# Full 128x128 stationaries for the small products of an RWKV-7 recurrence

## The chip, the cores and the metric

The kernel runs on one core of a Trainium2 chip. The metric is device microseconds of one execution, as the median of the runs. Matrix products run on TensorE (PE in the profile, its weight loads PEld), elementwise work on VectorE (DVE), ScalarE (ACT) and GpSimd (POOL); SyncE (SP) issues the DMAs.

## The reference

One hybrid decoder layer on 1024 tokens of width 1024, in float32: RMSNorm, one projection, a sliding-window attention branch and an RWKV-7 branch, both gated and merged, a hierarchical MoE and a last gated projection. The change touches the RWKV-7 branch, whose core is this scan over the tokens, for 8 heads of size 64:

```python
def step(state, inp):
    r_t, w_t, k_t, v_t, kk_t, a_t = inp
    sa = jnp.einsum('bhvk,bhk->bhv', state, -kk_t)
    state = (state * w_t[:, :, None, :]
             + sa[..., None] * (kk_t * a_t)[:, :, None, :]
             + v_t[..., None] * k_t[:, :, None, :])
    y_t = jnp.einsum('bhvk,bhk->bhv', state, r_t)
    return state, y_t
```

After it each head's output is normalised, scaled, gets a bonus term and is gated.

## The kernel before

The scan is done in chunks of 64 tokens, two chunks to a block of 128 tokens, 8 blocks. The 8 heads form 4 pairs `j`; in a pair, head `par` 0 lies on partitions 0 to 63 and head 1 on 64 to 127. `rwkv_block` (L654) writes for block `b`: the inputs of block b+1 (`rwkv_front`), chunk 0, the pairwise products of b+1 (`rwkv_pairs`, `rwkv_tokmajor`), chunk 1, the outputs (`rwkv_out`), and the inverse of b+1 (`rwkv_inverse`).

- `rwkv_pairs` (L469) multiplies `bk` with `stk`, masks the two PSUM banks into `ab` (two buffers) and `stk`, and sends the 16x16 diagonal blocks of `ab` (`xd`, `xc`) through DRAM to a forward substitution `T` (L503 to L507) and back as `dc`.
- `rwkv_inverse` (L538) makes the 64x64 inverse of each head and chunk in four rounds, (d,ab), (dt,e), (x,e), (x,e), each of 16 products with a 64x64 stationary, with an eviction by DVE between (L557, L566); the last gives `tt`.
- `rwkv_chunk` (L570) is the recurrence: z = stk.svu (8 products, stationary 128x64, L586), a copy `zs` by ACT, u = tt.zs (8, 64x64, L594), two copies of u into `svu`, the state pS = bkt.svu (8, 128x64, L602), `tmp` and the new `svu` by DVE, and the outputs: y1 = stk.svu (L589) and y2 = ab.svu (8, 64x64, L616), both into PSUM banks `py`, two for a block.
- `rwkv_out` (L618) reads `py` with DVE, normalises, transposes `yc` with 4 PE transposes and writes `yrT`.

A product in float32 shows as two MATMUL records, each with a weight load of its own. Between the small products `fill(n)` (L221) takes n steps of a generator of large products, three records each of 128x512 (`ps_mm<-h,wh` and `h,wl`, later `yah`, `yal`): the numbers of steps stand in `FN` (L30), 28 steps to a block. What is left of the generator runs after the last block (`branch_b`, L835). The Tile framework's scheduler makes a fixed order for each engine from priorities (program order, with the chunks pulled forward by `TN`) and the dependences; the engines then run in that order. PSUM tiles have tags with two buffers each: `mm`, `w`, `c`, `py`.

Of the kernel before, what the change touches and what calls it, by code (L numbers as in the profile page):

```python
# [37 lines left out]
_o = 0  # L38
# [8 lines left out]
for _n, _c in (("ident", 128), ("msk", 128), ("offm", 64), ("offt", 64), ("dm", 64), ("ind2", 2), ("i16", 256), ("tri", 128),  # L47
               ("bones", 128), ("band", 256), ("invf", 32)):
    CA[_n] = slice(_o, _o + _c)
    _o += _c  # L50
NCA = _o
CB = {}
# [19 lines left out]
class Kern:  # L72
# [157 lines left out]
    def rope_tables(self, pool):  # L230
        nc = self.nc
        MAGIC = 12582912.0
        n = 256
        pi = pool.tile([128, 8], I32, name="pos_i")
        nc.sync.dma_start(pi, self.a["positions"].rearrange("(t p) -> p t", p=128))
        pf = pool.tile([128, 8], F32, name="pos_f")
        nc.vector.tensor_copy(pf, pi)
        r = pool.tile([128, 8, 32], F32, name="rp_r")
        k = pool.tile([128, 8, 32], F32, name="rp_k")
        kh = pool.tile([128, 8, 32], F32, name="rp_kh")  # L240
        invf = self.ca[:, CA["invf"]]
# [12 lines left out]
        nc.vector.tensor_scalar(r, r, lim, -lim, op0=ALU.min, op1=ALU.max)  # L254
        sn = self.cos_sin[:, :, 1, :]
        nc.scalar.activation(self.cos_sin[:, :, 2, :], r, AF.Sin)
        nc.vector.tensor_scalar(self.cos_sin[:, :, 1, :], self.cos_sin[:, :, 2, :], -1.0, None, op0=ALU.mult)
        nc.vector.scalar_tensor_tensor(k, r, -1.0, r, op0=ALU.mult, op1=ALU.max)
        nc.vector.tensor_scalar(k, k, -1.0, math.pi / 2, op0=ALU.mult, op1=ALU.add)
        nc.scalar.activation(self.cos_sin[:, :, 0, :], k, AF.Sin)  # L260

    def att_block(self, n, ap):
# [50 lines left out]
        band = self.ca[:, CA["band"]][:, 256 - nk:]  # L313
# [53 lines left out]
    def rwkv_front(self, b, rp):  # L367
# [77 lines left out]
        for par in range(2):  # L445
            h = slice(par * 64, par * 64 + 64)
            nc.vector.tensor_tensor(bk[h, :, :, par, :], v4(na)[h], ei[h], op=ALU.mult)
            nc.vector.tensor_tensor(bk[h, :, :, 1 - par, :], v4(kp)[h], ei[h], op=ALU.mult)
            nc.vector.tensor_tensor(stk[h, :, :, par, 0:64], v4(kk)[h], ex[h, :, :, 0:64], op=ALU.mult)
            nc.vector.tensor_tensor(stk[h, :, :, par, 64:128], v4(r)[h], ex[h, :, :, 1:65], op=ALU.mult)  # L450
# [18 lines left out]
    def rwkv_pairs(self, b, st, rp):  # L469
# [3 lines left out]
        ab = rp.tile([128, 2, 4, 128], F32, name="ab", bufs=2)  # L473
        msk = self.ca[:, CA["msk"]]
        mb = lambda q: msk[q, None, :].to_broadcast([64, 4, 128])
        hs = [slice(0, 64), slice(64, 128)]
        for c in range(2):
# [11 lines left out]
        st["ab"] = ab  # L489
        dA, dT = self.dA[b % 2], self.dT[b % 2]  # L490
        x = rp.tile([128, 2, 4, 64], F32, name="xd", tag="f", bufs=5)
        nc.vector.tensor_tensor(x, ab[:, :, :, 0:64], self.ca[:, CA["dm"]][:, None, None, :].to_broadcast([128, 2, 4, 64]),
                                op=ALU.mult)
# [3 lines left out]
        sa = rp.tile([64, 16, 16], F32, name="sa", bufs=1)  # L497
# [13 lines left out]
        dc = rp.tile([128, 16, 16], F32, name="dc", bufs=1)  # L511
# [26 lines left out]
    def rwkv_inverse(self, b, st, rp):  # L538

        nc = self.nc  # L540
        ab, dc = st["ab"], st["dc"]
        shp = [128, 2, 4, 64]
        bc4 = lambda m: self.ca[:, CA[m]][:, None, None, :].to_broadcast(shp)
        f = lambda p: p.rearrange("p (c a t) -> p c a t", c=2, a=4)
        heads = [(c, j, slice(par * 64, par * 64 + 64)) for c in range(2) for j in range(4) for par in range(2)]
        n = lambda name: rp.tile(shp, F32, name=name, tag="td", bufs=4)
# [5 lines left out]
        e = n("e")  # L552
        p = self.ptile("c")
        for c, j, h in heads:
            self.mm(f(p)[h, c, j, :], ab[h, c, j, 0:64], d[h, c, j, :])
        self.fill(FN["in0"])
        nc.vector.tensor_tensor(e, f(p), bc4("offm"), op=ALU.mult)  # L557

        x = dt
        for i in range(3):  # L560
            p = self.ptile("c")
            for c, j, h in heads:
                self.mm(f(p)[h, c, j, :], e[h, c, j, :], x[h, c, j, :])
            self.fill(FN["in1"])
            x = n("x") if i < 2 else rp.tile(shp, F32, name="tt", bufs=2)
            nc.vector.tensor_tensor(x, f(p), dt, op=ALU.add)  # L566
        tt = x
        st["tt"] = tt

    def rwkv_chunk(self, b, c, st, nxt, rp):  # L570
        nc = self.nc
        stk, ab, bkt, tt = st["stk"], st["ab"], st["bkt"], st["tt"]
        if c == 0:
            st["py"] = [self.ptile("py") for _ in range(2)]
        fy = [p[:, :256].rearrange("p (a v) -> p a v", a=4) for p in st["py"]]
        f = lambda p: p[:, :256].rearrange("p (a v) -> p a v", a=4)
        svu = st["svu"][c]
# [21 lines left out]
        if not last:  # L599
            pS = self.ptile("c")  # L600
            for j, par, h in heads:
                self.mm(f(pS)[h, j, :], bkt[c][:, j, par * 64:par * 64 + 64], svu[:, j, par, :])  # L602
# [6 lines left out]
            nc.vector.tensor_tensor(tmp, self.sm, f(pS), op=ALU.add)  # L609
            ns = st["svu"][1] if c == 0 else nxt["svu"][0]  # L610
            for par in range(2):
                h = slice(par * 64, par * 64 + 64)
                nc.vector.tensor_tensor(ns[h, :, par, :], tmp[h], fc[h].to_broadcast([64, 4, 64]), op=ALU.mult)
            nc.gpsimd.tensor_tensor(self.sm, tmp, fc.to_broadcast([128, 4, 64]), op=ALU.mult)
        for j, par, h in heads:
            self.mm(fy[par][out, j, :], ab[h, c, j, 64:128], svu[h, j, par, :], start=False, stop=j == 3, skip=True)  # L616

    def rwkv_out(self, b, st, rp):  # L618

        nc = self.nc  # L620
        fy = [p[:, :256].rearrange("p (a v) -> p a v", a=4) for p in st["py"]]
        g = lambda n: rp.tile([128, 4, 128], F32, name=n, tag="g", bufs=2)
        st8 = rp.tile([128, 8], F32, name="st8", bufs=2)
        yc = g("yc").rearrange("p a (q v) -> p a q v", q=2)
        s2 = st8.rearrange("p (a q) -> p a q", q=2)
        for par in range(2):
            nc.vector.tensor_reduce(s2[:, :, par], fy[par], op=ALU.add, axis=AX.X)
# [12 lines left out]
        for j in range(4):  # L640
            self.tr(p[:, j * 128:(j + 1) * 128], yc[:, j].rearrange("p q v -> p (q v)"))
# [102 lines left out]
    def mixer(self):  # L744
# [802 lines left out]
def host_consts():  # L1547
# [19 lines left out]
    ca[:, CA["band"]] = np.where(np.concatenate([s[None] > p[:, None], s[None] <= p[:, None]], 1), 0.0, -1e30)  # L1567
    ca[:, CA["invf"]] = np.float32(10000.0 ** (-np.arange(32) / 32))[None]
# [10 lines left out]
    return ca, cb  # L1579


def host_arrays(inputs):
# [18 lines left out]
    a["ca"], a["cb"] = host_consts()  # L1601
# [3 lines left out]
INS = ["x", "p", "positions", "vec", "ca", "cb", "w_in", "w0", "w_decay_up", "w_aaa_up", "w_gate_up", "sinks",  # L1605
# [22 lines left out]
```

## Time and profile before

| | |
|---|---|
| median of 3 runs (lowest to highest) | 1700.5 us (1698.99 to 1700.76) |
| the profiled execution's own time | 1698.45 us |
| its span in the profile | 1696.6 us |
| PE busy | 1618.1 us (95%), 9856 records |
| DVE busy | 1279.7 us (75%) |
| ACT busy | 863.0 us (51%) |
| granted TensorE clock, mean | 0.98 of 2.4 GHz |

Busy times are unions of the intervals of an engine's instructions. A matmul's record lasts longer than its turn, since matmuls are pipelined: what a record costs in a row of records is the time from its start to the next record's start. The timeline view merges neighbours of one kind, with the count behind an x.

### The profile page before, as it was taken

To read this page: it belongs to the slowest core of one execution; us is meant where nothing else is said; L and a number is where in the kernel's file an instruction comes from. 1 tells how busy PE (TensorE), PEld (TensorE's weight loads), DVE (VectorE), ACT (ScalarE), POOL (GpSimd) and SP (SyncE) were. 2 spreads that over 40 slices of the span, in tenths; PEclk is the share of its full clock that TensorE was granted. 3 is DMA by queue.
4 is the path that set the end of the run, shared out by engine and by line. 5 is a ranking of instruction groups with operands and counts; after the bars stand their busy time and mean duration, and the time that the engine had idled before them with its cause. 6 is when DMAs were issued, how large, how long until landed. Compare 5 with 4: busy or idle time off the path is not lost.

```text
span 1696.6 us, 26475 instructions
## 1 busy us (share of the span) xinstructions
PE 1618.1 (95%) x9856; PEld 1225.6 (72%) x9856; DVE 1279.7 (75%) x2636; ACT 863.0 (51%) x1389; POOL 156.5 (9%) x134
## 2 busy tenths in 40 slices
PE   7999999999999999999899699999999999999697
PEld 5877777777787878778687466666666666666586
DVE  7256665377788888666608889999998888899785
ACT  5234333332233333322313388888887777888442
POOL 1000000000000000000002312112211111111000
PEclk9999999999999999999999899999999999999799
DMA  6333222332323323368837689999799989999651
GB/s 191 103 108 100 70 74 82 109 100 79 78 55 94 79 76 88 110 212 267 262 113 265 226 311 335 384 372 380 286 360 349 346 300 349 344 386 362 218 175 50
DMA packets 189030, 349.75 MB, mean 206 GB/s; under 512 B 50862, under 2 KB 123182, under 8 KB 164322
## 3 DMA queue, kind: packets, MB, share of 16 engines
q1 hardware_dynamic: 179682, 331.02, 56.3%
q0 software_dynamic: 9216, 17.01, 3.2%
q8 instruction: 78, 1.28, 0.3%
q14 instruction: 54, 0.44, 0.1%
HBM read 301.10 MB, written 52.95 MB: 209 GB/s over the span
## 4 chain that ended last, share of the span: by engine, by line
PE 81%; DVE 9%; DMA 5%; issue 2%; ACT 2%; SPq 1%; POOL 0%; DVEq 0%; ACTq 0%; POOLq 0%
PE ps_mm L77 47%; PE ps_py L77 16%; PE ps_c L77 9%; PE ps_w L81 4%; PE ps_w L77 4%; PE ps_c L81 1%; DVE so L1068 1%; DMA raw<-in_w_out_dram 1%; DMA ysp<-yaT 1%; DMA mraw<-in_w_up_e_dram 1%; DMA x<-in_x_dram 0%; DMA zr<-zT 0%; DVE wl L1187 0%; ACT sm L337 0%; DMA yb<-y,idx 0%
## 5 line engine op out<-in xcount | busy, mean ns | idle before, releaser
L1187 DVE TENSOR_TENSOR wl<-mraw,wh 128x1024 fp32r<-128x1024 f32 x384 | 457.8, 1220 | 51.0 <-ACT wh L1186 49.9
L1186 ACT ACTIVATE wh<-mraw 128x1024 fp32r<-128x1024 f32 x384 | 402.7, 1058 | 96.0 <-PE ps_mm L77 66.2
L77 PE MATMUL ps_mm<-h,wh 128*128 128x512 f32 x1152 | 378.7, 403 | 0.1
L77 PEld LDWEIGHTS ps_mm<-h,wh 128*128 128x128 f32 x1152 | 214.3, 189 | 47.4 <-issue 1.6
L77 PE MATMUL ps_mm<-h,wl 128*128 128x512 f32 x576 | 231.1, 401 | 0.0
L77 PE MATMUL ps_mm<-wh,xh 128*88 128x512 f32 x512 | 205.3, 401 | 0.0
L77 PE MATMUL ps_mm<-wl,xh 128*88 128x512 f32 x512 | 204.1, 399 | 1.3 <-DVE wl L1187 1.2
L77 PE MATMUL ps_mm<-wh,xl 128*88 128x512 f32 x512 | 201.8, 394 | 0.0
L77 PEld LDWEIGHTS ps_mm<-h,wl 128*128 128x128 f32 x576 | 108.8, 189 | 23.4 <-issue 1.0
L1244 POOL DMA_INDIRECT yb<-y,idx x32 | 71.4, 2230 | 462.6 <-ACT wh L1186 255.0
L77 PEld LDWEIGHTS ps_mm<-wl,xh 128*88 128x88 f32 x512 | 79.4, 155 | 40.5 <-DVE wl L1187 5.0
L77 PEld LDWEIGHTS ps_mm<-wh,xl 128*88 128x88 f32 x512 | 79.4, 155 | 37.2 <-DVE xl L1163 0.2
L77 PEld LDWEIGHTS ps_mm<-wh,xh 128*88 128x88 f32 x512 | 79.3, 155 | 35.0 <-issue 0.4
L77 PE MATMUL ps_py<-wl,hh 128*88 128x512 f32 x256 | 102.7, 401 | 0.0
L77 PE MATMUL ps_py<-wh,hl 128*88 128x512 f32 x256 | 100.3, 393 | 0.5 <-DVE hl L1228 0.5
L77 PE MATMUL ps_py<-wh,hh 128*88 128x512 f32 x256 | 99.4, 393 | 0.6 <-ACT hh L1227 0.6
L102 ACT ACTIVATE wh<-raw 128x1024 fp32r<-128x1024 f32 x44 | 46.6, 1058 | 100.4 <-PE ps_mm L77 95.2
L103 DVE TENSOR_TENSOR wl<-raw,wh 128x1024 fp32r<-128x1024 f32 x42 | 51.3, 1220 | 60.9 <-ACT wh L102 60.5
L77 PEld LDWEIGHTS ps_py<-wl,hh 128*88 128x88 f32 x256 | 39.4, 154 | 27.2 <-DVE wl L1187 10.0
L77 PEld LDWEIGHTS ps_py<-wh,hh 128*88 128x88 f32 x256 | 39.5, 154 | 20.4 <-ACT hh L1227 0.7
L77 PEld LDWEIGHTS ps_py<-wh,hl 128*88 128x88 f32 x256 | 39.5, 155 | 17.9 <-DVE hl L1228 0.9
L77 PE MATMUL ps_mm<-woh,m 128*128 128x512 f32 x128 | 47.0, 417 | 1.3 <-ACT m L93 1.3
(398 smaller groups left out, 2877.5 us busy)
## 6 DMA issues: line engine op xcount, KB each, us to landing
mraw<-in_w_gate_e_dram SPq DMA_DIRECT2D x64, 1024.0 KB, 8.8
mraw<-in_w_up_e_dram SPq DMA_DIRECT2D x64, 1024.0 KB, 8.6
mraw<-in_w_down_e_dram SPq DMA_DIRECT2D x64, 1024.0 KB, 8.5
raw<-in_w_in_dram SPq DMA_DIRECT2D x36, 512.0 KB, 4.1
gT<-t SPq DMA_DIRECT2D x32, 256.0 KB, 2.0
g<-gT SPq DMA_DIRECT2D x32, 256.0 KB, 4.5
yin<-yb SPq DMA_DIRECT2D x16, 512.0 KB, 5.2
zT<-t SPq DMA_DIRECT2D x28, 256.0 KB, 2.0
```

What stands on the lines that cost most here:

```text
L77: return self.nc.tensor.matmul(out, l, r, start=start, stop=stop, skip_group_check=skip)
L81: return self.nc.tensor.transpose(out, in_, self.ident[:k, :k])
L102: nc.scalar.activation(wh, raw, AF.Copy)
L103: (eng or nc.vector).tensor_tensor(wl, raw, wh.bitcast(F32), op=ALU.subtract)
L1068: V.tensor_scalar(so, cb[:, CB["iota"]][:, :CAP], pk[:, k:k + 1], None, op0=ALU.is_equal)
L1186: nc.scalar.activation(wh, r, AF.Copy)
L1187: nc.vector.tensor_sub(wl, r, wh.bitcast(F32))
L1244: nc.gpsimd.indirect_dma_start(out=self.yb[:, :], out_offset=bass.IndirectOffsetOnAxis(ap=sidx, axis=0), in_=y, in_offset=None, bounds_che ...
```

## The change

Products of the inverse and of u take both heads of a pair as one 128x128 block diagonal stationary (`abd`, `ttb`); z and y1 become one product with the whole 128 columns of `stk`, into `py`; pS and y2 take 128 columns of weights and 128 moving columns, both heads of a pair at once (y2 with `abx`, whose blocks lie off the diagonal; of pS the two diagonal blocks are read). The halves of `stk` and the rows of `py` swap places for head 1, one `py` bank serves one chunk, and the outputs are put in order by 16 products with 64x64 stationaries in place of the 4 transposes. `abd` and `ttb` have one buffer, `abx` two; all four are zeroed once by POOL. The mask `offt` is applied where `abd` is written, instead of `offm` after the first round. `band` and `invf` move from the constants `ca` to a tensor `ct` of their own, loaded into the attention's pool; `sa` and `dc` share one buffer, and the `td` tag has 3 buffers for 4.

```diff
@@ rwkv_pairs
-                nc.vector.tensor_tensor(ab[h, c], pv[h], mb(h), op=ALU.mult)
-                nc.vector.tensor_tensor(stk[o, :, c, par, :], pv[o], mb(o), op=ALU.mult)
+                nc.vector.tensor_tensor(x[h, c], pv[h, :, h], cm(h, "dlt"), op=ALU.mult)
+                nc.vector.tensor_tensor(abd[h, c, :, h], pv[h, :, h], cm(h, "offt"), op=ALU.mult)
+                nc.vector.tensor_tensor(stk[o, :, c, par, :], pv[o], mb(o, par), op=ALU.mult)
+                nc.vector.tensor_tensor(abx[h, c, :, o], pv[h, :, o], mb(h, 0)[:, :, 64:128], op=ALU.mult)
-        nc.vector.tensor_tensor(x, ab[:, :, :, 0:64], self.ca[:, CA["dm"]][:, None, None, :].to_broadcast([128, 2, 4, 64]),
-                                op=ALU.mult)
@@ rwkv_inverse
-        for c, j, h in heads:
-            self.mm(f(p)[h, c, j, :], ab[h, c, j, 0:64], d[h, c, j, :])
+        for c, j in pairs:
+            self.mm(f(p)[:, c, j, :], abd[:, c, j, :], d[:, c, j, :])
         self.fill(FN["in0"])
-        nc.vector.tensor_tensor(e, f(p), bc4("offm"), op=ALU.mult)
+        for h in HS:
+            nc.scalar.activation(abd[h, :, :, h], f(p)[h], AF.Copy)
...
-            for c, j, h in heads:
-                self.mm(f(p)[h, c, j, :], e[h, c, j, :], x[h, c, j, :])
+            for c, j in pairs:
+                self.mm(f(p)[:, c, j, :], abd[:, c, j, :], x[:, c, j, :])
             self.fill(FN["in1"])
-            x = n("x") if i < 2 else rp.tile(shp, F32, name="tt", bufs=2)
-            nc.vector.tensor_tensor(x, f(p), dt, op=ALU.add)
+            if i < 2:
+                x = n("x")
+                nc.vector.tensor_tensor(x, f(p), dt, op=ALU.add)
+            else:
+                for h in HS:
+                    nc.vector.tensor_tensor(self.ttb[h, :, :, h], f(p)[h], dt[h], op=ALU.add)
@@ rwkv_chunk
-        for j, par, h in heads:
-            self.mm(f(pz)[h, j, :], stk[:, j, c, par, 0:64], svu[:, j, par, :])
+        for j in range(4):
+            for par in range(2):
+                self.mm(fy[:, j, par, :], stk[:, j, c, par, :], svu[:, j, par, :], start=j == 0 and par == 0, stop=False, skip=True)
         self.fill(FN["ch0"])
-        for j, par, h in heads:
-            self.mm(fy[par][out, j, :], stk[:, j, c, par, 64:128], svu[:, j, par, :], start=j == 0, stop=False, skip=True)
-        nc.scalar.activation(zs, f(pz), AF.Copy)
+        for par, h in enumerate(HS):
+            nc.scalar.activation(zs[h], fy[h, :, par, :], AF.Copy)
-        for j, par, h in heads:
-            self.mm(f(pu)[h, j, :], tt[h, c, j, :], zs[h, j, :])
+        for j in range(4):
+            self.mm(f(pu)[:, j, :], ttb[:, c, j, :], zs[:, j, :])
...
-            for j, par, h in heads:
-                self.mm(f(pS)[h, j, :], bkt[c][:, j, par * 64:par * 64 + 64], svu[:, j, par, :])
+            for j in range(4):
+                self.mm(pS[:, j * 128:j * 128 + 128], bkt[c][:, j, :], svu[:, j].rearrange("p q v -> p (q v)"))
...
-            nc.vector.tensor_tensor(tmp, self.sm, f(pS), op=ALU.add)
+            for par, h in enumerate(HS):
+                nc.scalar.activation(tmp[h], f2(pS)[h, :, par, :], AF.Copy)
+            nc.vector.tensor_tensor(tmp, self.sm, tmp, op=ALU.add)
...
-        for j, par, h in heads:
-            self.mm(fy[par][out, j, :], ab[h, c, j, 64:128], svu[h, j, par, :], start=False, stop=j == 3, skip=True)
+        for j in range(4):
+            self.mm(py[:, j * 128:j * 128 + 128], abx[:, c, j, :], svu[:, j].rearrange("p q v -> p (q v)"),
+                    start=False, stop=j == 3, skip=True)
@@ rwkv_out
+        for c in range(2):
+            fy = st["py"][c].rearrange("p (a q v) -> p a q v", a=4, q=2)
+            for par in range(2):
+                nc.scalar.activation(ycf[HS[1 - par], 4 * c:4 * c + 4, :], fy[HS[1 - par], :, par, :], AF.Copy)
+        nc.vector.tensor_reduce(st8, ycf, op=ALU.add, axis=AX.X)
...
         for j in range(4):
-            self.tr(p[:, j * 128:(j + 1) * 128], yc[:, j].rearrange("p q v -> p (q v)"))
+            for c in range(2):
+                for par, h in enumerate(HS):
+                    o = HS[1 - par]
+                    self.mm(p[h, j * 128 + c * 64:j * 128 + c * 64 + 64], ycf[o, 4 * c + j, :], self.ident[o, o])
```

## Rows read from the trace of the kernel before

**Rows 1.** Windows, 389 to 735 us: length, busy PE, PEld, DVE, ACT, POOL, clock, DMA

```profile
389.00:735.00 346.00, 340.04 (x3437) 271.24 (x3438) 272.95 (x781) 113.12 (x245) 15.06 (x33) 1.00 0.32 86
```

**Rows 2.** Timeline, PE: one round of the inverse (start us, us, what)

```profile
484.07 0.63 PE L77 MATMUL ps_mm<-h,wh 128*128 128x512 f32 x2
484.63 1.15 PE L77 MATMUL ps_c<-dt,e 64*64 64x64 f32 x32
485.71 0.50 PE L77 MATMUL ps_mm<-h,wl 128*128 128x512 f32 x1
486.04 0.62 PE L77 MATMUL ps_mm<-h,wh 128*128 128x512 f32 x2
486.51 0.40 PE L77 MATMUL ps_mm<-h,wl 128*128 128x512 f32 x1
```

**Rows 3.** Timeline, PE: products of two chunks

```profile
508.97 1.15 PE L77 MATMUL ps_py<-svu,stk 128*64 128x64 f32 x16
...
555.72 0.69 PE L77 MATMUL ps_c<-svu,bkt 128*64 128x64 f32 x16
556.33 0.68 PE L77 MATMUL ps_py<-svu,ab 64*64 64x64 f32 x16
556.95 0.50 PE L77 MATMUL ps_mm<-h,wh 128*128 128x512 f32 x1
```

**Rows 4.** Timeline, PE: full-width float32 products beside large ones

```profile
515.68 0.95 PE L77 MATMUL ps_w<-ca,sq 128*128 128x2 f32 x8
516.49 0.48 PE L77 MATMUL ps_mm<-h,wl 128*128 128x512 f32 x1
516.81 0.40 PE L77 MATMUL ps_mm<-h,wh 128*128 128x512 f32 x1
517.05 0.60 PE L81 MATMUL ps_c<-ident,yc 128*128 128x128 f32 x4
517.49 1.06 PE L77 MATMUL ps_c<-xg,wg 128*128 128x128 f32 x8
518.30 0.48 PE L77 MATMUL ps_mm<-h,wh 128*128 128x512 f32 x1
```

**Rows 5.** Lines by form, PE: the changed products, whole span (busy, mean ns | idle before)

```profile
L77 PE MATMUL ps_c<-x,e 64*64 64x64 f32 x512 | 20.9, 222 | 0.3
...
L77 PE MATMUL ps_py<-svu,stk 128*64 128x64 f32 x256 | 19.6, 225 | 0.0
L77 PE MATMUL ps_py<-svu,ab 64*64 64x64 f32 x256 | 18.5, 226 | 0.0
...
L77 PE MATMUL ps_c<-svu,bkt 128*64 128x64 f32 x240 | 14.1, 230 | 0.4 <-ACT svu L596 0.4
L77 PE MATMUL ps_c<-svu,stk 128*64 128x64 f32 x256 | 13.6, 229 | 0.2
...
L77 PE MATMUL ps_c<-zs,tt 64*64 64x64 f32 x256 | 10.9, 224 | 0.2 <-DVE tt L566 0.2
L77 PE MATMUL ps_c<-dt,e 64*64 64x64 f32 x256 | 9.8, 230 | 1.1 <-DVE e L557 1.1
L77 PE MATMUL ps_c<-d,ab 64*64 64x64 f32 x256 | 9.2, 221 | 0.8 <-DVE d L551 0.8
```

**Rows 6.** Tiles tt and zs: evictions (ns min/median/max, first to last start)

```profile
L566 DVE TENSOR_TENSOR tt<-ps_c,dt x8: 690/692/694, 391.7 to 721.4; 128x512 f32<-128x512 f32 x8
...
L591 ACT ACTIVATE zs<-ps_c x16: 366/383/383, 390.7 to 730.7; 128x256 f32<-128x256 f32 x16
```

**Rows 7.** Tile cos_sin: the rope table's first use and its end

```profile
L272 DVE TENSOR_TENSOR ra<-ps_w,cos_sin x16: 283/487/692, 93.6 to 266.5; 128x512 f32<-128x512 f32 x8, 128x128 f32<-128x128 f32 x8
...
L260 ACT ACTIVATE cos_sin<-rp_k x1: 407/407/407, 50.6 to 50.6; 128x256 f32<-128x256 f32 x1
```

**Rows 8.** Tiles xc and e: the pairs' last step, the inverse's last rounds

```profile
L495 DVE TENSOR_REDUCE xc<-xd x8: 1010/1024/1048, 354.2 to 683.4; 128x128 f32<-128x512 f32 x8
...
L77 PE MATMUL ps_c<-x,e x512: 218/218/268, 387.7 to 721.1; 64*64 64x64 f32 x171
```

More of the change, by code (lines that the diff above doesn't have):

```diff
@@ L46 @@
 _o = 0
-for _n, _c in (("ident", 128), ("msk", 128), ("offm", 64), ("offt", 64), ("dm", 64), ("ind2", 2), ("i16", 256), ("tri", 128),
-               ("bones", 128), ("band", 256), ("invf", 32)):
+for _n, _c in (("ident", 128), ("msk", 192), ("dlt", 64), ("offt", 64), ("dm", 64), ("ind2", 2), ("i16", 256), ("tri", 128),
+               ("bones", 128)):
     CA[_n] = slice(_o, _o + _c)
@@ L51 @@
 NCA = _o
+CT = {}
+_o = 0
+for _n, _c in (("band", 256), ("invf", 32)):
+    CT[_n] = slice(_o, _o + _c)
+    _o += _c
+NCT = _o
+HS = [slice(0, 64), slice(64, 128)]
 CB = {}
@@ L312, in att_block @@
         mx = ap.tile([128, 8], F32, name="mx", bufs=2)
[L313 removed]
+        band = self.ct[:, CT["band"]][:, 256 - nk:]
         for jj in range(2):
@@ L448, in rwkv_front @@
             nc.vector.tensor_tensor(bk[h, :, :, 1 - par, :], v4(kp)[h], ei[h], op=ALU.mult)
-            nc.vector.tensor_tensor(stk[h, :, :, par, 0:64], v4(kk)[h], ex[h, :, :, 0:64], op=ALU.mult)
-            nc.vector.tensor_tensor(stk[h, :, :, par, 64:128], v4(r)[h], ex[h, :, :, 1:65], op=ALU.mult)
+            nc.vector.tensor_tensor(stk[h, :, :, par, HS[par]], v4(kk)[h], ex[h, :, :, 0:64], op=ALU.mult)
+            nc.vector.tensor_tensor(stk[h, :, :, par, HS[1 - par]], v4(r)[h], ex[h, :, :, 1:65], op=ALU.mult)
         st["stk"], st["bk"] = stk, bk
@@ L472, in rwkv_pairs @@
         bk, stk = st["bk"], st["stk"]
-        ab = rp.tile([128, 2, 4, 128], F32, name="ab", bufs=2)
+        abd, abx = self.abd, self.abx[b % 2]
         msk = self.ca[:, CA["msk"]]
-        mb = lambda q: msk[q, None, :].to_broadcast([64, 4, 128])
-        hs = [slice(0, 64), slice(64, 128)]
+        mb = lambda q, par: msk[q, None, par * 64:par * 64 + 128].to_broadcast([64, 4, 128])
+        cm = lambda q, n: self.ca[q, None, CA[n]].to_broadcast([64, 4, 64])
+        hs = HS
+        x = rp.tile([128, 2, 4, 64], F32, name="xd", tag="f", bufs=5)
         for c in range(2):
@@ L540, in rwkv_inverse @@
         nc = self.nc
-        ab, dc = st["ab"], st["dc"]
+        abd, dc = self.abd, st["dc"]
         shp = [128, 2, 4, 64]
-        bc4 = lambda m: self.ca[:, CA[m]][:, None, None, :].to_broadcast(shp)
         f = lambda p: p.rearrange("p (c a t) -> p c a t", c=2, a=4)
-        heads = [(c, j, slice(par * 64, par * 64 + 64)) for c in range(2) for j in range(4) for par in range(2)]
-        n = lambda name: rp.tile(shp, F32, name=name, tag="td", bufs=4)
+        pairs = [(c, j) for c in range(2) for j in range(4)]
+        n = lambda name: rp.tile(shp, F32, name=name, tag="td", bufs=3)
         d, dt = n("d"), n("dt")
@@ L561, in rwkv_inverse @@
             p = self.ptile("c")
-            for c, j, h in heads:
-                self.mm(f(p)[h, c, j, :], e[h, c, j, :], x[h, c, j, :])
+            for c, j in pairs:
+                self.mm(f(p)[:, c, j, :], abd[:, c, j, :], x[:, c, j, :])
             self.fill(FN["in1"])
-            x = n("x") if i < 2 else rp.tile(shp, F32, name="tt", bufs=2)
-            nc.vector.tensor_tensor(x, f(p), dt, op=ALU.add)
-        tt = x
-        st["tt"] = tt
+            if i < 2:
[4 more added lines that the diff above has]
+                    nc.vector.tensor_tensor(self.ttb[h, :, :, h], f(p)[h], dt[h], op=ALU.add)
     def rwkv_chunk(self, b, c, st, nxt, rp):
         nc = self.nc
[L572 to L575, printed above, removed]
+        stk, abx, bkt, ttb = st["stk"], st["abx"], st["bkt"], self.ttb
+        py = self.ptile("py")
+        st["py"] = st.get("py", []) + [py]
         f = lambda p: p[:, :256].rearrange("p (a v) -> p a v", a=4)
+        f2 = lambda p: p.rearrange("p (a q v) -> p a q v", a=4, q=2)
+        fy = f2(py)
         svu = st["svu"][c]
@@ L618, in rwkv_out @@
     def rwkv_out(self, b, st, rp):
         nc = self.nc
-        fy = [p[:, :256].rearrange("p (a v) -> p a v", a=4) for p in st["py"]]
         g = lambda n: rp.tile([128, 4, 128], F32, name=n, tag="g", bufs=2)
         st8 = rp.tile([128, 8], F32, name="st8", bufs=2)
[L624 to L627, printed above, removed]
+        ycf = g("yc").rearrange("p a (q v) -> p (a q) v", q=2)
@@ L640, in rwkv_out @@
         for j in range(4):
-            self.tr(p[:, j * 128:(j + 1) * 128], yc[:, j].rearrange("p q v -> p (q v)"))
+            for c in range(2):
+                for par, h in enumerate(HS):
+                    o = HS[1 - par]
+                    self.mm(p[h, j * 128 + c * 64:j * 128 + c * 64 + 64], ycf[o, 4 * c + j, :], self.ident[o, o])
         yT = g("yT")
@@ L768, in mixer @@
             self.stage_b_qkv(hh, hl, 2)
+            self.ct = ap.tile([128, NCT], F32, name="ct")
+            nc.sync.dma_start(self.ct, self.a["ct"])
             self.cos_sin = ap.tile([128, 8, 3, 32], F32, name="cos_sin")
@@ L776, in mixer @@
             sts = {}
+            self.abd = rp.tile([128, 2, 4, 128], F32, name="abd")
+            self.abx = [rp.tile([128, 2, 4, 128], F32, name=f"abx{i}") for i in range(2)]
+            self.ttb = rp.tile([128, 2, 4, 128], F32, name="ttb")
+            for t in (self.abd, *self.abx, self.ttb):
+                nc.gpsimd.memset(t, 0.0)
             self.filler = chain(self.stage_b_gates(hh, hl), self.lazy(self.branch_a))
@@ L1566, in host_consts @@
     s = np.arange(128)
-    ca[:, CA["band"]] = np.where(np.concatenate([s[None] > p[:, None], s[None] <= p[:, None]], 1), 0.0, -1e30)
-    ca[:, CA["invf"]] = np.float32(10000.0 ** (-np.arange(32) / 32))[None]
+    ct = np.zeros((128, NCT), np.float32)
+    ct[:, CT["band"]] = np.where(np.concatenate([s[None] > p[:, None], s[None] <= p[:, None]], 1), 0.0, -1e30)
+    ct[:, CT["invf"]] = np.float32(10000.0 ** (-np.arange(32) / 32))[None]
     cb = np.zeros((128, NCB), np.float32)
@@ L1578, in host_consts @@
     cb[:, CB["jrow"]] = np.arange(NOV)[None]
-    return ca, cb
+    return ca, cb, ct
 def host_arrays(inputs):
@@ L1600, in host_arrays @@
     a["ln_final"] = g("ln_final")
-    a["ca"], a["cb"] = host_consts()
+    a["ca"], a["cb"], a["ct"] = host_consts()
     return a
-INS = ["x", "p", "positions", "vec", "ca", "cb", "w_in", "w0", "w_decay_up", "w_aaa_up", "w_gate_up", "sinks",
+INS = ["x", "p", "positions", "vec", "ca", "cb", "ct", "w_in", "w0", "w_decay_up", "w_aaa_up", "w_gate_up", "sinks",
        "w_branch_att", "w_branch_rwkv", "w_out", "ln_moe_k", "w_group", "b_group", "w_expert", "b_expert",
```

29 lines of the change are left out of this document (10 added, 19 removed).

## The prediction

> **What bounds the kernel now.** I began with the page's busy shares: PE is busy 95% of the span, the next engine, DVE, 75%. The question is whether PE is also the bound where the change is made. The windows view of the recurrence's blocks answers it: in 346 us PE is busy 340 and idle 6.0, its clock granted in full, while DVE is busy 273 and ACT 113 [rows 1]. There is always a large product of the generator to put between two small ones, so PE never rests, and each microsecond of PE's work that is added or taken away there should show in the time. The matmul's own duration says little about that; the timeline does, which gives a record's turn as the distance to the next start. Lines by form give counts and the sums to hold it against.
>
> A large record has a turn of 0.235 us: two of them fill 486.04 to 486.51 [rows 2]. In front of a round of the inverse two take 0.56 instead of 0.47, so entering a group of narrow products costs 0.10. In front of a full-width float32 group one takes 0.24, so entering that costs nothing [rows 4]. The first large record after a group takes 0.33 behind narrow products [rows 2] and 0.32 behind full-width ones [rows 4]: leaving costs the same in both.
>
> **The change on PE.** Each product is two records, each with its own weight load. Before:
> - A round of the inverse is 32 records in 1.08 us (484.63 to 485.71), 0.034 each: the two heads lie in opposite corners of the array, and their records run side by side. With the entry 1.18, and 32 rounds (4 in each of 8 blocks): 37.8 us.
> - z has the form of pS: 16 records in 0.61 [rows 3]; with the entry 0.71, 16 chunks: 11.4. pS, 15 chunks: 10.7. u has the inverse's form, half a round (0.54) to y2's 0.62; with 0.61 and the entry 11.4.
> - y1: 1.15 less the tail of 0.07 that pS also shows beyond its turn (0.69 against 0.61), so 1.08 [rows 3]; with the entry 1.18 by 16, 18.9. It is dearer than z because both heads write the same half of the rows.
> - y2 takes 0.62 at best [rows 3], but its busy time of 18.5 is 1.16 a chunk [rows 5]; less the tails I take 16.5 for all.
> - The four transposes take 0.44 a block (517.05 to 517.49) [rows 4]: 3.5.
> Together 110.2 us.
>
> After, the stationaries have 128 columns. Such a record is not in the trace with 64 moving columns, but it is bracketed closely: 8 records take 0.81 with 2 moving columns and 0.81 with 128 (517.49 to 518.30) [rows 4], so 0.101 each whatever moves. It is the load of the weights that sets the pace, and a zero half of a block diagonal matrix is loaded like the rest.
> - A round: 8 products, 16 records, 1.62; 32 rounds: 51.8.
> - z with y1: 16 records, 1.62; 16 chunks: 25.9. u, 8 records, 0.81: 13.0. pS: 12.2. y2: 13.0.
> - The outputs: 32 narrow records for 4 transposes, as one round with entry, 1.18 by 8: 9.4.
> Together 125.3, that is 15.1 more. The number of products falls from 148 to 88 a block, but the work falls only where heads did not run side by side (y1, y2); in the inverse one wide load of 0.202 a pair replaces four narrow records of 0.135.
>
> The other end: the busy sums of the changed products are 116.6 [rows 5]; with entries for 95 groups (9.5; I give y2, which mostly follows pS, none) and the transposes before is 129.6, and after is 4.3 **less**. But those sums count each group's tail of 0.07, some 8 us. The truth lies nearer the timeline, whose plain groups however miss the second entries where the scheduler splits a group. I take +11, with -4 and +15 as ends.
>
> **Waits added.**
> - After the first round two ACT copies of half the partitions replace one DVE product. zs, half as wide, takes 0.38 [rows 6]; two of twice the width lie between 0.77 and 1.53, against 0.69 of the tt form. Six large records (1.41) cover the round; without them it is PE's wait in full. 0 to 3 us in 8 blocks; 0.5 taken.
> - ttb: two DVE additions of 0.69 for one. u of the next chunk waits for them, behind it on PE the rest of the chunk. 0 to 5.5; I take 1.5, since the pairs of the next block and the round's fill stand there.
> - zs becomes two copies (+0.38), and two copies stand ahead of tmp (+0.77): 1.15 a chunk on the chain of the state, 17 us in 15 chunks if nothing covered it. PE's idle of 6.0 [rows 1] says that it is covered now. A gain is possible too: z leaves the c banks, which the inverse also uses. -3 to 17; +1 taken, near the covered end.
> - Pairs: four reads of a bank instead of two, three of half width (0.35 to 0.69 by the tt row), less xd: about +1.6 us of DVE a block, 13 in all, DVE then at some 286 of 360. Costed at nothing: the generator covers it; without that cover the second half's products wait for the w banks.
> - The outputs' ACT copies and the longer path at the end lie beside the generator's rest; nothing. On SP, ct is one more transfer ahead of the positions, and ca is smaller: the rope table is ready at 50.6 and first read at 93.6 [rows 7], 43 us of cover. The four memsets on POOL fall between the attention's end, after 266.5 [rows 7], and the first pairs, shortly before 354.2 [rows 8]; nothing. The DMAs of a block are the same, each queue's order too.
>
> Sum: 11 + 0.5 + 1.5 + 1 = **+14 us** on the profiled execution's 1698.45, so 1712.5; that execution was 2.05 below the median shown, so against the median I say **1714 us**. Something over 0.2%, 3.4 us, is what a measurement here can tell from no change.
>
> **The rivals.**
> 1. *The modes cost more than the rows show (faster).* If a change between narrow and wide products empties the array at both ends, the price is up to what a large record lasts beyond its turn, 0.40 - 0.235 = 0.16 [rows 2], at 222 ends: 35.5 us to win, against 24.6 of added records (125.3 less 110.2 without its 9.5 of entries), so -11: **1690**. It decides once an end costs over 0.11. For it: the 0.10 at entry. Against: the first large record behind a full-width group is as slow as behind a narrow one. The Trainium skill (TensorEngine Tiling (Array Packing), Key Properties) says that changing the tiling mode drains TensorE; the rows agree for the entry, 0.10 a time, and show nothing of it at the exit. Chance 0.13.
> 2. *The single abd buffer closes a loop (slower still).* The pairs of b+1 may write abd only when block b's last round has read it, and hold the w banks until then; ab had two buffers. From xc to the last round is 37.7 us in the last block (683.4 to 721.1), and a block takes 47.0 (354.2 to 683.4, seven blocks) [rows 8]. From the last round to the next xc I estimate 6 us (16 records of at least 1.6, some 2 of reads, 1.0 of xc, hand-overs); the rounds grow by 2.2 and ttb by 0.7: 46.6, against a block of 48.4 then. It decides when queueing adds over 2 us; with 6 it costs 4 by 7 blocks, 28: **1742**. Chance 0.13.
> 3. *No change.* PE's added work is paid from waiting that the busy time hides, z no longer stands between the inverse's rounds, and the -4 end of the sum holds with some waits: **1701**. Chance 0.11.
>
> **How the numbers follow.** The forecast has 0.63. Its own range is 1705 to 1724, from the ends of the record sum, mostly the upper half, and of the waits. Slower is forecast and rival 2, 0.76; no change 0.11; faster 0.13. The range 1698 to 1736 leaves out rival 1 and the upper half of rival 2, 0.19 together.
>
> **What would show it.** In the profile after: a round of (x,abd) 16 records 1.6 us long; (svu,stk) the same; groups of 8 records 0.8; large records in front of them without the 0.10; some 920 records fewer, at more PE time in the stage; the block's period 48 to 49 us; PE idle in the blocks below 12 us. Wrong it would be if 128-column records with 64 moving columns had a turn under 0.08, if the weight loads hid between large records because the scheduler spreads the products singly, or if PE idle in the blocks grew by tens of microseconds (rival 2, seen as waits of PE on abd's or the pairs' DVE work).

## The result, and the profile after

The change makes the kernel slower: 1739.41 us as the median of four runs (1737.63 to 1740.58) against 1699.74 (1697.80 to 1700.76) for the kernel before beside it, a ratio of 1.0234 [1.0216, 1.0252]. The forecast had the direction and the mechanism, but +14 us where +40 came; 1739 lies outside the range of 1698 to 1736.

The page's first part, after:

```profile
span 1737.8 us, 24767 instructions
PE 1657.2 (95%) x8936; PEld 1275.8 (73%) x8936; DVE 1297.5 (75%) x2676; ACT 902.0 (52%) x1483; POOL 160.9 (9%) x138
```

PE has 920 records fewer, as foretold, and is busy 39 us longer; its share is 95% as before. The windows view after (length, busy PE, PEld, DVE, ACT, POOL, clock, DMA), first the stretch of [rows 1], then the end of the stage. (The stage is the time from the first record of the inverse to the last of y2.)

```profile
389.00:735.00 346.00, 342.41 (x2352) 292.15 (x2352) 266.57 (x746) 135.88 (x308) 14.49 (x32) 0.99 0.26 69
740.00:800.00 60.00, 53.05 (x315) 43.43 (x310) 31.77 (x70) 17.10 (x33) 0.85 (x1) 0.89 0.54 172
```

In the blocks PE is idle 3.6 us, less than before: no wait has taken over, PE simply has more to do. Its weight loads (PEld) rise from 271 to 292 us although a third of the records is gone. Most of the idle time stands in the second window, at the end of the stage. The timeline after shows the products themselves, in this order: a round of the inverse, u, the state, the outputs' second part, z with y1.

```profile
499.35 1.89 PE L84 MATMUL ps_c<-x,abd 128*128 128x64 f32 x16
501.05 0.48 PE L84 MATMUL ps_mm<-h,wl 128*128 128x512 f32 x1
...
503.45 1.00 PE L84 MATMUL ps_c<-zs,ttb 128*128 128x64 f32 x8
504.38 1.16 PE L84 MATMUL ps_w<-stk,bk 64*128 64x128 f32 x8
...
506.03 1.05 PE L84 MATMUL ps_c<-svu,bkt 128*128 128x128 f32 x8
506.92 1.06 PE L84 MATMUL ps_py<-svu,abx 128*128 128x128 f32 x8
...
518.20 2.02 PE L84 MATMUL ps_py<-svu,stk 128*128 128x64 f32 x16 [0.17 <-ACT svu L545]
520.03 0.48 PE L84 MATMUL ps_mm<-h,wh 128*128 128x512 f32 x1
```

A round of 16 records takes 1.70 us (499.35 to 501.05), where 32 narrow records took 1.08 [rows 2]. Eight records take 0.89 from 506.03 to 506.92, with 128 moving columns; 16 with 64 moving columns take 1.83 (518.20 to 520.03). **The turn of a full-width record is 0.111 us**, whatever moves: 0.89/8, or the difference of 1.70 and the 0.81 of [rows 4] by the 8 records between them. The 0.101 of the prediction came from groups of 8 with a large record behind, whose last record has a turn of only some 0.03: 7 x 0.111 + 0.03 is the 0.81 seen there. The rows before held the right turn as well: the four transposes of [rows 4], which another full-width group follows, take 0.44, that is 0.110 each.

Lines by form after (busy, mean ns | idle before) answer to [rows 5]:

```profile
L84 PE MATMUL ps_py<-svu,stk 128*128 128x64 f32 x256 | 33.8, 278 | 3.0 <-DVE svu L625 1.4 <-ACT svu L545 0.8
L84 PE MATMUL ps_c<-x,abd 128*128 128x64 f32 x256 | 31.1, 275 | 0.1
L84 PE MATMUL ps_c<-zs,ttb 128*128 128x64 f32 x128 | 17.6, 283 | 0.1
L84 PE MATMUL ps_c<-d,abd 128*128 128x64 f32 x128 | 17.2, 293 | 0.0
L84 PE MATMUL ps_py<-svu,abx 128*128 128x128 f32 x128 | 16.9, 275 | 0.0
L84 PE MATMUL ps_c<-svu,bkt 128*128 128x128 f32 x120 | 16.6, 283 | 0.0
L84 PE MATMUL ps_c<-dt,abd 128*128 128x64 f32 x128 | 15.8, 277 | 0.0
L84 PE MATMUL ps_c<-ident,yc 64*64 64x64 f32 x256 | 9.2, 221 | 0.4 <-DVE yc L651 0.4
```

Half the records, more busy time: the last two rounds of the inverse, (x,abd), 31.1 for 20.9. Busy sums count a group's tail, so for the balance I added up, in the timeline of each kernel, the distance from each entry to the next one's start, from the first record of the inverse to the last of y2. Us by group (these sums are worked out from the whole timeline; a few records are missing in each; a wait counts to the entry in front of it; PE's other groups, 79 to 87 us of the stage, aren't listed). The last two rows give how much of the stage PE was idle, and how much of it had the lower clock:

| group | before | after | inverse narrow (e1) | all narrow (e3) | y layout, z in py (b4) |
|---|---|---|---|---|---|
| inverse | 38.3 | 59.2 | 36.8 | 36.5 | 36.7 |
| z and y1 | 25.5 | 29.5 | 28.6 | 17.8 | 18.4 |
| u | 10.8 | 15.3 | 15.0 | 12.9 | 9.8 |
| pS | 12.3 | 14.2 | 14.4 | 13.0 | 13.0 |
| y2 | 16.5 | 14.6 | 14.8 | 13.7 | 13.8 |
| transposes or their products | 3.2 | 7.6 | 7.5 | 10.0 | 7.5 |
| large, gate columns (h) | 154.8 | 153.3 | 165.2 | 171.3 | 156.0 |
| large, branch A (yah, yal) | 10.5 | 23.4 | 15.4 | 25.8 | 7.3 |
| whole stage | 351.4 | 396.8 | 378.3 | 387.7 | 341.6 |
| of it, PE idle | 5.7 | 8.8 | 10.2 | 14.3 | 3.9 |
| of it, at 1.2 GHz | 3.4 | 20.5 | 13.7 | 27.3 | 0 |

The changed products are 33.7 us dearer, 20.9 of it in the inverse. The stage is 45.4 longer; 7.4 of that comes back behind it (961.8 us to the end before, 954.4 after), since 27 large records of the generator moved into the stage; 3.2 us are lost ahead of it (it begins at 386.6 us, before at 383.4), and what they come from isn't shown. The rest lies at the end of the stage, in the timeline after:

```profile
742.69 0.40 PE L84 MATMUL ps_mm<-h,wl 128*128 128x512 f32 x1
745.00 0.50 PE L84 MATMUL ps_mm<-yah,wh 128*128 128x512 f32 x1 [1.91 <-ACT yah L100]
746.89 0.50 PE L84 MATMUL ps_mm<-yal,wh 128*128 128x512 f32 x1 [1.39 <-DVE yal L101]
748.33 0.79 PE L84 MATMUL ps_mm<-yah,wh 128*128 128x512 f32 x1 [0.70 <-ACT yah L100]
...
752.46 0.80 PE L84 MATMUL ps_mm<-yah,wh 128*128 128x512 f32 x1 [2.19 <-ACT yah L100]
...
755.48 3.51 PE L84 MATMUL ps_c<-d,abd 128*128 128x64 f32 x16
```

Here the generator changes from the gate columns to the next weights' branch, whose operands yah and yal are late; PE waits three times for over 1 us, and behind the waits the granted clock is the lower level, 1.2 GHz, for a while: a large record lasts 0.63 to 0.80 instead of 0.40, and a round 3.51 instead of 1.89. The copies that write yah wait for the load of their operand:

```profile
747.64 0.63 ACT L100 ACTIVATE yah<-ysp 128x512 fp32r<-128x512 f32 x1 [2.69 <-DMA ysp<-yaT]
```

SP issued the first load of ysp at 740.29 and the next at 744.58, behind stores of the gate columns and of yT. In the kernel before, three were issued from 709.56 to 712.30, and rounds of the last inverse stand between the last h record (710.21) and the first of yah (715.09); after, nothing of PE's work stands there.

The stage has two stretches at the lower clock. In the windows view:

```profile
669.40:676.20 6.80, 6.80 (x27) 6.00 (x27) 3.34 (x6) 1.44 (x4) 0.00 (x0) 0.50 0.04 6
747.90:761.50 13.60, 10.99 (x32) 8.33 (x33) 5.25 (x8) 5.23 (x9) 0.00 (x0) 0.50 0.81 227
```

The first has no wait in front of it: from 663.04 to 669.84 PE ran small products only, without a large record between them and without a gap. One block later the same kind of stretch, 719.81 to 726.41, kept the full clock. Some 2.8 us of the products' 140.3 are the clock's and not the columns' (0.6 of the 106.6 before): a round of the inverse took 3.27 for 1.70, a u 1.60 and a pS 1.45 for 0.89.

### The profile page after: what moved, and what is told of

The parts are those of the page before. It is cut to its first block, busy times and chain, and to the rows that moved or that the text cites. A ratio compares the mean times of both kernels' runs of the same rounds, so it can differ in the third digit from the quotient of the medians.

```text
span 1737.8 us, 24767 instructions
## 1 busy us (share of the span) xinstructions
PE 1657.2 (95%) x8936; PEld 1275.8 (73%) x8936; DVE 1297.5 (75%) x2676; ACT 902.0 (52%) x1483; POOL 160.9 (9%) x138
## 4 chain that ended last, share of the span: by engine, by line
PE 78%; DVE 11%; DMA 5%; ACT 3%; issue 2%; SPq 1%; DVEq 0%; ACTq 0%
PE ps_mm L84 44%; PE ps_py L84 16%; PE ps_c L84 10%; PE ps_w L88 4%; PE ps_w L84 4%; PE ps_c L88 1%; DMA raw<-in_w_out_dram 1%; DVE so L1091 1%; DMA mA<-g 1%; DVE svu L625 1%; ACT tmp L622 0%; DMA sinks<-in_sinks_dram 0%; DVE T L517 0%; DVE sub L515 0%; DVE wl L1210 0%
## 5 line engine op out<-in xcount | busy, mean ns | idle before, releaser
L956 ACT ACTIVATE jk<-x 128x512 f32<-128x512 f32 x16 | 10.1, 631 | 74.8 <-DVE x L954 37.2
```

Source lines behind the costliest of these rows:

```text
L956: nc.scalar.activation(jk, x, AF.Square, accum_out=sq[i][:, n:n + 1])
```

## The experiments

**Which of the products costs, and why (e1, e2).** Both take the inverse alone out of the change, in two ways: e1 with 64x64 stationaries cut from the same tile, e2 with all 128 rows, zeros included, but 64 columns.

```diff
e1:  -  self.mm(f(p)[:, c, j, :], abd[:, c, j, :], x[:, c, j, :])
     +  for h in HS:
     +      self.mm(f(p)[h, c, j, :], abd[h, c, j, h], x[h, c, j, :])
...
e2:  +  for h in HS:
     +      self.mm(f(p)[h, c, j, :], abd[:, c, j, h], x[:, c, j, :])
```

> The changed kernel with the inverse's rounds back to 64x64 stationaries, cut out of the block diagonal tile; all else as changed. Weight loads (the turn of a record follows the columns of its stationary, 0.111 us for 128): the inverse's groups fall from 59 us to some 39, the time from 1739 to 1717 to 1723. Loop through the single abd buffer, and the hand-overs in halves: both are still there, so 1735 to 1742.

> The changed kernel with the inverse's rounds on 128x64 stationaries: all 128 rows of the block diagonal tile, half of its columns at a time, 16 products a round. Weight loads set by the columns: a round takes 32 records at 0.038, 1.22, as z did before, so the time is within 5 us of e1 (1718 to 1728). If it is the full rows, the zeros or the missing corners of the array that cost: no gain over the changed kernel, 1735 to 1745. Loop: 1735 to 1742.

Measured: e1 1718.88 us, 1.0135 [1.0102, 1.0169] to the kernel before; e2 1716.68, 1.0117 [1.0078, 1.0156]. They are the same within their spread (e2 stands a hair under its range), and 20.5 and 22.7 under the kernel after; beside the kernel before the loss falls from 39.7 to 21.8 and 19.6. The timeline of e2:

```profile
488.45 1.15 PE L84 MATMUL ps_c<-x,abd 128*64 128x64 f32 x32
489.54 0.93 PE L84 MATMUL ps_w<-stk,bk 64*128 64x128 f32 x8
```

32 records in 1.09 us, as with 64 rows [rows 2]. So zeros and rows cost nothing; the columns do. Two heads in different column halves run side by side at 0.034 a record; as one wide stationary they took 0.111 a record. The Trainium skill (TensorE: Matmul & The Clock Gate, LDWEIGHTS) says that a weight load's time goes by its columns alone. e2 bears that out. An estimate by the Trainium skill's formula in that section, 107 ns for 128 columns, is close to the 111 measured.

**The same from the other side (b1).** The kernel before, with the last three of the four rounds wide in halves written by DVE, and nothing else of the change but fewer buffers, which make the room.

```diff
-  nc.vector.tensor_tensor(e, f(p), bc4("offm"), op=ALU.mult)
+  for h in (slice(0, 64), slice(64, 128)):
+      nc.vector.tensor_tensor(self.ebd[h, :, :, h], f(p)[h], om, op=ALU.mult)
...
-  self.mm(f(p)[h, c, j, :], e[h, c, j, :], x[h, c, j, :])
+  self.mm(f(p)[:, c, j, :], self.ebd[:, c, j, :], x[:, c, j, :])
```

> The kernel before with one part of the change: three of the inverse's four rounds, (dt,e), (x,e), (x,e), on 128x128 block diagonal stationaries, which DVE writes in two halves; to make room sa and dc, and xc and sub, share a buffer. Weight loads: 24 rounds of 1.78 in place of 1.18 us, 14 us more, so 13 to 18 over before. If the cost of the change sits in its other parts (z in py, copies in halves, the output's order, fewer buffers): within 3 us of before.

Measured: 1721.91, 1.0139 [1.0120, 1.0159], +24 us. The inverse grows by 16.2 us; 24 rounds by 0.62 (1.70 less 1.08) are 14.9. All six groups of products together grow by 18.4, y2 by 2.4 of it, and 6.4 us more are a wait for yah at the stage's end, which the kernel before doesn't have. So the time lies above the 13 to 18 expected, but the wide rounds cost nearly what they should in this kernel too.

**The single buffer (e4).** Two abd buffers, abx compact to make room, which makes y2 narrow.

```diff
-  self.abd = rp.tile([128, 2, 4, 128], F32, name="abd")
+  self.abd = [rp.tile([128, 2, 4, 128], F32, name=f"abd{i}") for i in range(2)]
```

> The changed kernel with two abd buffers by turns, as ab had; to make room y2 takes its 64x64 blocks from a half as wide abx. Weight loads: y2 alone gains 3 to 6 us, so 1733 to 1737. Loop through the single abd buffer: 10 to 30 us less, 1709 to 1729.

Measured: 1739.86, 1.0262 [1.0235, 1.0289], the time of the kernel after. The second buffer gains nothing, and no wait for abd stands in the kernel after, so rival 2 is out. The 3 to 6 us expected of y2 didn't come either: narrow, it takes 13.8 us of the stage for 14.6.

**All products narrow again (e3, e8).** e3 keeps the changed layout (swapped halves of stk, one py bank a chunk, four reads of a pair's bank) and makes every product narrow. e8 goes on from it: abd (two buffers), abx and ttb without zero blocks, evictions of whole partitions, sa and dc apart, four td buffers.

```diff
e3:  -  self.mm(f(pu)[:, j, :], ttb[:, c, j, :], zs[:, j, :])
     +  for h in HS:
     +      self.mm(f(pu)[h, j, :], ttb[h, c, j, h], zs[h, j, :])
...
e8:  -  for h in HS:
     -      nc.scalar.activation(abd[h, :, :, h], f(p)[h], AF.Copy)
     +  nc.scalar.activation(abd, f(p), AF.Copy)
```

> The changed kernel's layout with every product narrow again: inverse, u and the outputs y2 with 64x64, z, y1 and the state with 128x64 stationaries, z and y1 as two groups whose heads alternate between the halves of the rows; the state is added from PSUM by DVE again. Weight loads: inverse -20, z and y1 together -8, u -4.5, y2 and the state -8, so about 1699 (1693 to 1706), all that was lost comes back. Loop and hand-overs: 1730 or more.

> e3 with the buffers and evictions as before: abd, abx and ttb as 64 wide tiles, abd in two buffers, one eviction over all partitions for abd and ttb, sa and dc apart, four td buffers. What is left over the kernel before is z in py with two copies, four reads of a bank in the pairs, and the output's order. If fewer buffers and the halves cost e3 its 26 us: 1690 to 1705. If the cost is in z, the pairs or the output: 1715 to 1727, as e3.

Measured: e3 1723.51, 1.0157 [1.0133, 1.0181]; e8 1713.04, 1.0111 [1.0081, 1.0140]. Both miss the time of before, and e3 both of its forecasts, though the products are back at its cost or under (the table: 103.9 us for the six groups of e3, 106.6 before). e3 is even 4.6 us slower than e1, whose groups take 117.1. The time is now in waits and in the clock, as the last rows of the table say. The buffers and the evictions in halves, which e8 takes back, are worth 10.5 us there, less than the 18 or more expected if they were all of it. The timeline of e3, where the next block's front begins:

```profile
514.25 0.40 PE L84 MATMUL ps_mm<-h,wl 128*128 128x512 f32 x1
517.03 1.10 PE L84 MATMUL ps_w<-wdw,xw 65*128 65x512 f32 x2 [2.38 <-issue]
517.56 1.34 PE L84 MATMUL ps_mm<-h,wh 128*128 128x512 f32 x2
518.70 0.63 PE L84 MATMUL ps_mm<-h,wl 128*128 128x512 f32 x1
```

PE stands before the product wdw of xw. Behind the wait large records run at the lower clock for some 3 us. The same trace shows what the wait ends with: SP's issue of a load, and ACT's copy, which waits for it.

```profile
509.36 0.37 SPq L380 DMA_DIRECT2D zr<-zT  x1
516.62 0.31 ACT L393 ACTIVATE xw<-zr 64x128 f32<-64x128 f32 x1 [2.46 <-DMA zr<-zT]
```

The tile zr has one buffer, and its load is issued as soon as the transposes of the last block's zr are done (here they end at 509.3). From then on the load and the copy run against the work that PE has left in front of wdw. The waits view of PE from 384 to 735 us (us in total, times, longest) has this wait as its first row, in e3:

```profile
PE ps_w L84 <- issue: 10.7, 6, 2.8
```

In e8 it is no smaller:

```profile
PE ps_w L84 <- issue: 12.0, 6, 2.6
```

The same view of the kernel after has three rows, and wdw is not among them:

```profile
PE ps_py L84 <- DVE svu L625: 1.1, 5, 0.3
PE ps_py L84 <- ACT svu L545: 0.8, 3, 0.3
PE ps_w L84 <- DVE rk L462: 0.7, 3, 0.4
```

So the parts of the change have a second cost beside the products, which doesn't show in the kernel after.

**Where the second cost is (b2, b5).** b2 is the kernel before with the new output layout alone: each head's y on its own rows, one py bank a chunk, 16 narrow products (32 records) in place of the four transposes. b5 is b2 with the four DVE reads of a pair's bank (xd straight from PSUM, without ab's mask).

```diff
b2:  -  self.mm(fy[par][out, j, :], stk[:, j, c, par, 64:128], svu[:, j, par, :], start=j == 0, stop=False, skip=True)
     +  self.mm(fy[h, j, :], stk[:, j, c, par, 64:128], svu[:, j, par, :], start=j == 0, stop=False, skip=True)
...
b5:  -  nc.vector.tensor_tensor(ab[h, c], pv[h], mb(h), op=ALU.mult)
     +  nc.vector.tensor_tensor(x[h, c], pv[h, :, 0:64], dmh, op=ALU.mult)
     +  nc.vector.tensor_tensor(ab[h, c, :, 0:64], pv[h, :, 0:64], mb(h)[:, :, 0:64], op=ALU.mult)
     +  nc.vector.tensor_tensor(ab[h, c, :, 64:128], pv[h, :, 64:128], mb(h)[:, :, 64:128], op=ALU.mult)
```

> The kernel before with the outputs' layout alone: y1 and y2 stay narrow but write the rows of their own head into one py bank a chunk, so that the heads run side by side, and 16 products with 64x64 stationaries replace the four transposes. By the turns: y1 -7, y2 -3 to -6, output +5, so 4 to 8 us faster than before (1690 to 1694). If the output's order is what brings waits (e3's 26 us): 5 to 20 us slower.

> b2 with four DVE reads of each pair bank in place of two, as in the change (the diagonal blocks, the two halves of ab, and stk; the diagonal blocks unmasked below the diagonal, which T does not read). 1.6 us more of DVE a block, the w banks held longer. If that is the rest in e3 and e8: 6 to 20 us over b2. If not: within 3 us of b2.

Measured: b2 1698.68, 1.0005 [0.9992, 1.0018], no change, neither the gain nor the loss expected; b5 1706.58, 1.0051 [1.0035, 1.0067], 8 us over b2. In the waits view of b5 the wait before wdw is there again, 7.0 us:

```profile
PE ps_w L77 <- issue: 7.0, 6, 2.5
```

The pairs' reads were costed at nothing in the prediction, with the generator as cover. With narrow products they cost 8 us. Two times of each block tell where, medians of seven blocks worked out from the timelines: from the issue of zr's load to the end of xw, and PE's work between the transposes of zr and wdw.

| us | before | after | b2 | b5 | e3 | e8 |
|---|---|---|---|---|---|---|
| load of zr and copy xw | 6.4 | 6.5 | 6.0 | 6.7 | 7.5 | 7.2 |
| PE's work meanwhile | 6.8 | 6.8 | 6.0 | 6.1 | 6.0 | 5.9 |

In b5, e3 and e8 the load and its copy take longer than the work that covers them; from b2 to b5 only the load's side grows. How four reads by DVE lengthen it isn't shown. In e8 some 7.6 us stand beyond the reads (15.6 over the kernel before beside it, less 8); the wait before wdw is 5.0 longer than in b5, and the rest stays unexplained.

**The end of the stage (g1).** The kernel after with one step of the generator fewer at two places of each block, so that the gate columns would last longer.

```diff
-FN = dict(fr0=2, fr1=2, fr2=2, fr3=2, fr4=2, pr0=1, ch0=1, ch1=1, ch2=1, in0=2, in1=2)
+FN = dict(fr0=2, fr1=1, fr2=2, fr3=2, fr4=1, pr0=1, ch0=1, ch1=1, ch2=1, in0=2, in1=2)
```

> The changed kernel with one large step less behind two of the front's products (fr1 and fr4 at 1): 16 steps, 48 large records, 11 us of them, move from the blocks to behind the last one. In the changed kernel the change from the gate columns to branch A in the stream of large products meets no other work of PE: it waits there for yah and yal, and its clock falls. If that is some of the loss, the last inverse now covers it and the time falls by 5 to 10 us, to 1729 to 1735. If only the weight loads count: within 3 us of the changed kernel.

Measured: 1743.71, 1.0276 [1.0260, 1.0291], 4 us slower. In 740 to 800 us the granted clock is 0.89 as in the kernel after, and the same waits stand there. But the edit didn't do what it was meant to: the last h record starts at 742.15 (742.69 in the kernel after), the last inverse only at 757.13, and the stage holds 653 large records for 642. So whether the last inverse would cover the change of operands was not put to the test, and what would cure it isn't shown.

**A version that beats both (b3, b4).** b3 is b2 with y1 directly behind z, as the change has it. In b4 z goes into the free half of the chunk's py bank as well, as in the change, instead of a c bank; all stationaries stay narrow.

```diff
b3:     self.mm(f(pz)[h, j, :], stk[:, j, c, par, 0:64], svu[:, j, par, :])
     -  self.fill(FN["ch0"])
        ...
        self.mm(fy[h, j, :], stk[:, j, c, par, 64:128], svu[:, j, par, :], start=j == 0, stop=False, skip=True)
     +  self.fill(FN["ch0"])
b4:  -  pz = self.ptile("c")
     +  pz = py[:, 256:512]
```

> b2 with y1 directly behind z and the large step after both: one entry less a chunk, 1.6 us, and the copy zs covered as before. By the turns 1 to 3 us faster than b2, 1694 to 1698, so faster than both kernels by a hair or the same as before. If PE's waits decide now and not its turns: no gain over b2.

> b3 with z in the chunk's py bank instead of a c bank, as in the change. If z in py is what costs e3 and e8 their rest of 15 to 26 us: 8 us or more over b3. If not: within 3 us of b3.

Measured: b3 1697.46, 1.0001 [0.9991, 1.0011]; b4 1687.27, **0.9946 [0.9931, 0.9961]**, 0.5% faster than the kernel before. Neither expectation for b4 held, 8 us over b3 or the same: z in py gains 10 us here, so z in py by itself is not what costs e3 and e8 their rest. The timeline of b4, z and y1 of one chunk:

```profile
555.62 0.40 PE L77 MATMUL ps_mm<-h,wh 128*128 128x512 f32 x1
555.95 1.15 PE L77 MATMUL ps_py<-svu,stk 128*64 128x64 f32 x32
557.03 0.50 PE L77 MATMUL ps_mm<-h,wh 128*128 128x512 f32 x1
```

The tile view of b4, the pairs' last step, answers to [rows 8]:

```profile
L495 DVE TENSOR_REDUCE xc<-xd x8: 1015/1032/1046, 354.1 to 679.0; 128x128 f32<-128x512 f32 x8
```

z and y1 of a chunk are one group of 32 records in 1.08 us, with one entry; the wide product takes 1.83 for the same. The blocks' period is 46.4 us ((679.0 less 354.1)/7) against 47.0. b2 and b3 have the cheaper outputs too (z and y1 19.5 us in b2), but pay for it elsewhere: PE waits for DVE's work on the inverse and the outputs (d 2.3 us, yc 1.8, x 1.1 in b2; x 1.7 and yc 0.8 in b4). One tile of the c banks fewer in each chunk goes with fewer such waits; that this is the cause is argued, not shown alone.

## Why the prediction was wrong

The step that failed is the record sum on PE, taken at +11 us. By the timeline it is 33.7 for the products, less 1.5 for the large records. The cover at the end of the stage, taken as given, failed beside it, 6.5 us.

**Right**: PE is the bound in these blocks, so PE's added work showed in the time nearly one for one (33.7 us of products in a difference of 39.7). The load of a stationary's columns sets the pace, zeros included; the sign by part held for the inverse, u, the state and the transposes' products, which got dearer, and for y2, which got cheaper. It did not hold for z with y1. PE idle in the blocks fell to 3.6 us, under the 12 given as the mark, and the ACT copies, the halves of ttb and the state's chain cost no more than the 3 us taken: waits in the stage before its end are 2.6 us. POOL, SP and the rope table cost nothing that shows.

**Wrong, in the order of size:**
- *The turn of a wide record and the counts.* "0.101 each whatever moves" should have been 0.111. For some 1144 records of the stage that is 11.4 us. Without entries the prediction had 100.7 before and 124.5 after, 23.8 apart; the timeline gives 106.6 and 140.3, so 33.7. This term is 9.9 short: the loss after was read from groups that end in front of a large record. The price before was read from the plainest groups and was too low as well, by 5.9, which hid some of the error. By part, z with y1 is where even the sign was wrong: 27.0 to 25.9 without entries in the prediction, 25.5 to 29.5 in the timeline.
- *The entries.* Credited with 9.5 us for 95 groups. The price was right: the median turn of a large record in front of a group is 0.33 before narrow ones, and 0.235 in front of most wide ones. But only some 50 stretches of large records of the stage end in front of a narrow group before; 6 after. The other groups follow each other. That is some 4.4 us, and the large h records as a whole fell by 1.5, since waits counted to them (0.6 us more) and the lower clock of 669.4 to 676.2 us (some 1.3) took part of it.
- *The end of the stage.* The prediction had the generator as cover everywhere. Where the generator's own operands are late there is none: some 6.5 us of waits and lower clock (23.4 less 10.5, less 27 records by 0.235).
- *The shading from +15 to +11*, towards the busy sums of [rows 5]. Those sums said 4.3 less; the timeline's end was the true one, and itself too low.
- *The pairs' reads*, costed at nothing with the generator as cover, showed nothing in the kernel after. b5 gives them a price with narrow products, 8 us; that the slower products are their cover after is argued from this, not shown.

With the measured sizes the working gives 33.7 - 1.5 + 6.5 = 38.7 us, of 41.2 between the two profiled executions (39.7 between the medians). Most of the rest is the 3.2 ahead of the stage. The clock is in these sizes and had no term in the prediction.

**The rivals.** Rival 1 had the entry right (0.10), and nothing at the exit: the first large record behind a wide group takes 0.32 (501.05 to 501.37), as in [rows 4]. e1 shows its sign wrong: going back to narrow, with its entries, gains 20.5 us. Rival 3 is out by the interval of the ratio. Rival 2 fell by e4; the blocks' period did grow, to 53.0 us ((729.3 less 358.2)/7) where 48 to 49 were forecast, but through PE's own work. The tile view after:

```profile
L505 DVE TENSOR_REDUCE xc<-xd x8: 1025/1035/1059, 358.2 to 729.3; 128x128 f32<-128x512 f32 x8
```

**What stays open:** what would bring the loads of ysp earlier at the stage's end, or cover them; what lengthens zr's load behind four reads; the rest of e8; why b4's gain comes with the c bank; the 3.2 us ahead of the stage.

## What to carry to other kernels

Price a small product by the columns of its stationary, not by the number of products: merging two that already ran side by side took 1.6 times as long here (a round 1.70 us for 1.08). Of the merged parts only y2 got cheaper, 16.5 to 14.6, whose heads had stood behind each other, and there narrow products that write each head's own rows did more (13.8). Read a record's turn from inside a long group or from two groups of different length, not from a group closed by another kind of work. A term that is "covered" is only covered as long as the slower thing stays slow: keep its own price as a bound, since the four reads cost 8 us where the products were quick.

## What the runs showed of the hardware

- Stationaries with all 128 rows and different halves of the columns run side by side as well as those in opposite corners of the array: 32 records in 1.09 us (e2) and 1.08 [rows 2]. The Trainium skill (TensorE: Matmul & The Clock Gate, Part 3: Packing small matmuls) has loads overlap running products only where the row groups differ. Here the rows are the same and the records follow each other in 0.034 us, and the measurement decides.
- The waits of PE between large products cost more than their length: behind the 2.38 us in e3, and behind those of 1.91 and 1.39 us in the kernel after, records ran at 1.2 GHz, 0.63 us for a large one that takes 0.40, and a round 3.51 for 1.89.
- The clock can fall without a wait: in the kernel after it was granted at 0.50 from 669.4 to 676.2 us, behind 6.4 us of small products that left no gap. The same stretch one block later kept it.
